# Down projections of a two-layer decoder trunk: the high weight part multiplies both halves of y in one matmul, and VectorE adds two sums

## The chip, the cores and the metric

The kernel runs on one core of one Trainium2 chip. The metric is the device time of one launch in microseconds. Three runs of the kernel before took 623.03, 623.33 and 623.62 us: the median is 623.33 us. One execution more was taken with the hardware profiler; it took 622.74 us, of which 620.9 us are the span that the profile shows.

## The reference

The program computes two decoder layers over 256 positions of width 1024, all in 32-bit floating point, and a final RMS norm. Layer 0 mixes with block-sparse attention beside gated linear attention, layer 1 with a recurrent block. Each layer ends with the same feed-forward block, which is what the change touches:

```python
def conv_ffn(x, w_up, conv_w, conv_b, w_down):
    h = causal_dwconv(x @ w_up, conv_w, conv_b)
    u, g = jnp.split(h, 2, axis=-1)
    return (u * jax.nn.gelu(g)) @ w_down

h = h + conv_ffn(rms_norm(h, ffn_norm_g[l]), ffn_w_up[l], ffn_conv_w[l], ffn_conv_b[l], ffn_w_down[l])
```

The widths are 1024 into 6144 (`w_up`), and 3072 into 1024 (`w_down`). The product with `w_down` is called the down projection here.

## The kernel before

**Layout.** Activations are kept transposed: features on the 128 partitions, the 256 positions along the free dimension. `h`, the residual stream, is 8 blocks of 128 features by 256 positions.

**Products in two halves.** TensorE is fed operands of the type fp32r. Every operand a is split in a high half, the value rounded to that type, and a low half, a minus the high half. A product a·b is taken as high·high + high·low + low·high, all summed in one PSUM region. For weights, `issue_w` (L130) loads a chunk of 128 x 1024 values (eight blocks of 128 x 128) by DMA into a tile `w`; ScalarE copies it to `wh` (L145), and VectorE subtracts into `wl` (L146). For the activations of the down projection, `Y` (L667) holds 24 blocks `y`, each with its high half [.., 0, ..] beside its low half [.., 1, ..], 256 columns each. `passes` (L152) issues three matmuls for each block: `wh` with the high half, `wh` with the low half, `wl` with the high half (L157). Each matmul instruction carries its own load of the 128 x 128 weights.

**Chunks.** 204 chunks are consumed in a fixed order. Tiles `w` have 4 buffers, so that a load waits until VectorE has made the `wl` of an earlier chunk; `wh` and `wl` have 6 buffers each, so that a split waits until TensorE has used up an earlier chunk. The first ten chunks of the recurrent block (L1_C0, NPRE) have buffers of their own and are split ahead, while the down projection of layer 0 still runs.

**The down projection** (L690 to L700) runs over m, the 8 blocks of output features. Each m takes a PSUM bank `psd` of 512 columns, uses 256 of them, and sums 3 chunks of 8 blocks into it: 72 matmuls. Then `residual` (L224) lets VectorE add the bank to block m of `h` (L225), ScalarE take squares of the block for the next norm (L183) and write the high half of the next operand `x` (L219), and VectorE the low half (L220).

**The order.** Python only gives a priority. The order on each engine is made when the kernel is built, by a scheduler that goes by a timeline of its own, and each engine runs its queue in that order: what stands behind a waiting instruction waits with it. In the recurrent block that follows layer 0, TensorE first multiplies `x` into the banks `psx` (L717).

Of the kernel before, what the change touches and what calls it, by code (L numbers as in the profile page):

```python
# [22 lines left out]
P = 128  # L23
S = 256
D = 1024
KT = 8
# [36 lines left out]
def trunk(ctx: ExitStack, tc: tile.TileContext, xT, w, wgk, wgk2, vec, cst, mskf, out):  # L63
    nc = tc.nc
# [7 lines left out]
    def bank(name, tag="g"):  # L72
        return pp.tile([P, 512], F32, tag=tag, bufs=BANKS[tag], name=name)
# [7 lines left out]
    h = big[:, 0:KT * S].rearrange("p (k t) -> p k t", k=KT)  # L81
# [4 lines left out]
    def V(name, i):  # L86
        o = VOFF[name] + i
        return vt[:, o:o + 1]
# [8 lines left out]
    def use(name):  # L97
        if tbl["name"] != name:
            ld = nc.scalar.preload_act_table_set(name)  # L99
            for o in tbl["ops"]:  # L100
                order(o, ld)
            if tbl["load"] is not None and not tbl["ops"]:
                order(tbl["load"], ld)
            tbl.update(name=name, load=ld, ops=[])

    def act(name, *args, **kw):
        use(name)
        ins = nc.scalar.activation(*args, **kw)  # L108
        order(tbl["load"], ins)
        tbl["ops"].append(ins)  # L110
        return ins

    first = []
    state = {"hooks": {}, "i": 0, "q": []}
# [10 lines left out]
    def load_w():  # L125
        while len(state["q"]) <= LOOK and state["i"] < NCH:
            state["q"].append(issue_w())
        return state["q"].pop(0)

    def issue_w():  # L130
        i = state["i"]
        state["i"] += 1
        wt = wp.tile([P, CW + 32], F32, tag="w", name=f"w{i}")[:, 0:CW]
        dma = nc.sync.dma_start(wt, w[i])
        if i == 0:
            first.append(dma)
        pre = "p" if L1_C0 <= i < L1_C0 + NPRE else ""
        nb = NPRE if pre else 6
        oh, ol = 16, 16
        wh = wp.tile([P, CW + 32], F32R, tag="wh" + pre, bufs=nb, name=f"wh{i}")[:, oh:oh + CW]  # L140
        wl = wp.tile([P, CW + 32], F32R, tag="wl" + pre, bufs=nb, name=f"wl{i}")[:, ol:ol + CW]
        nsp = 2 if i < 2 else 1
        for f in range(nsp):
            cs = slice(f * CW // nsp, (f + 1) * CW // nsp)
            hi = nc.scalar.activation(wh[:, cs], wt[:, cs], AF.Copy)  # L145
            lo = nc.vector.tensor_sub(wl[:, cs], wt[:, cs], wh[:, cs].bitcast(F32))  # L146
        for kind, o in (("h", hi), ("l", lo)):
            for before in state["hooks"].pop((kind, i), []):
                order(before, o)
        return wh, wl  # L150

    def passes(ps, ops, first=True, last=True, skip=False):  # L152
        n = len(ops)
        out = []
        for i, (ah, al, bh, bl) in enumerate(ops):
            for j, (a, b) in enumerate(((ah, bh), (ah, bl), (al, bh))):
                out.append(nc.tensor.matmul(ps, a, b, start=first and i + j == 0, stop=last and i == n - 1 and j == 2,  # L157
                                            skip_group_check=skip))
        return out

    def gemm(ps, wc, X, k0=0, first=True, last=True, nk=KT, skip=False):
        return passes(ps, [(wc[0][:, k * P:(k + 1) * P], wc[1][:, k * P:(k + 1) * P], X[:, k0 + k, 0, :], X[:, k0 + k, 1, :])
                    for k in range(nk)], first, last, skip)

    def split(hi, lo, src):
        nc.scalar.activation(hi, src, AF.Copy)
        nc.vector.tensor_sub(lo, src, hi.bitcast(F32))  # L167

    def new_x():
        return xp.tile([P, KT, 2, S], F32R, tag="x", name="x")  # L170
# [122 lines left out]
    X = new_x()  # L293
# [8 lines left out]
    with tc.tile_pool(name="l0", bufs=1) as lp, tc.tile_pool(name="l0r", bufs=4) as lr:  # L302
# [50 lines left out]
        for n, (k, i) in enumerate(seq):  # L353
            mc = 32 - 16 * i
            nc.tensor.matmul(psg[0:mc, :S], gw[:, k, 0:mc], X[:, k, i, :], start=n == 0, stop=n == 2 * KT - 1,
                             skip_group_check=True)
# [27 lines left out]
        for wdt in (64, 16, 4):  # L384
            c = cum[wdt]
# [16 lines left out]
        ps = bank("psbq")  # L402
# [18 lines left out]
        ps = bank("psbk")  # L421
# [94 lines left out]
        for nm in ("q", "k"):  # L516
            for m in range(2):
                ps = bank("psa")
# [63 lines left out]
        for pr in range(4):  # L582
            for j, ps in enumerate(scores(pr)):
                PT[2 * pr + j] = softmax(ps)
            ps = bank("pso", "t")
            for j in range(2):
                hd = 2 * pr + j
                r = slice(64 * j, 64 * j + 64)
                cs = slice(64 * hd, 64 * hd + 64)
# [11 lines left out]
        for pr in range(4):  # L601
            ps = bank("pob", "l")
            for j in range(2):
# [3 lines left out]
                cs = slice(64 * hd, 64 * hd + 64)  # L607
# [9 lines left out]
        for m in range(4):  # L617
            ps = bank("psog")
# [23 lines left out]
        X = new_x()  # L642
# [21 lines left out]
    def ffn(layer, X, norm, nextg):  # L664
        rs = norm.rstd()
        with tc.tile_pool(name=f"f{layer}", bufs=1) as yp, tc.tile_pool(name=f"f{layer}r", bufs=3) as fr:
            Y = yp.tile([P, 24, 2, S], F32R, name="y2")  # L667
            for m in range(24):
                ps = bank("psu")
                for j in range(2):  # L670
                    gemm(ps[:, j * S:(j + 1) * S], load_w(), X)
                v = fr.tile([P, 2, S], F32, tag="v", name="v")
                nc.vector.tensor_mul(v, ps.rearrange("p (j t) -> p j t", j=2), rs[:, None, :].to_broadcast([P, 2, S]))  # L673
                c = fr.tile([P, 2, S], F32, tag="c", name="c")
                for j in range(2):
                    ch = j * 24 + m
                    wv = lambda tap: V("fc_w", layer * 144 + tap * 48 + ch)
                    nc.scalar.activation(c[:, j, :], v[:, j, :], AF.Identity, bias=V("fc_b", layer * 48 + ch), scale=wv(2))  # L678
                    for d in (1, 2):
                        nc.vector.scalar_tensor_tensor(c[:, j, d:], v[:, j, 0:S - d], wv(2 - d), c[:, j, d:],  # L680
                                                       op0=ALU.mult, op1=ALU.add)
                gl = fr.tile([P, S], F32, tag="gl", name="gl")
                act(GELU, gl, c[:, 1, :], AF.Gelu_apprx_tanh)
                y = fr.tile([P, S], F32, tag="y", name="y")
                nc.vector.tensor_mul(y, c[:, 0, :], gl)
                split(Y[:, m, 0, :], Y[:, m, 1, :], y)
            use(SQRT)
            Xn = new_x() if nextg else None
            nn = Norm(last=nextg is None)
            for m in range(KT):  # L690
                ps = bank("psd")
                for c in range(3):
                    state["last"] = gemm(ps[:, :S], load_w(), Y, k0=8 * c, first=c == 0, last=c == 2)[-1]
                add = residual(ps[:, :S], m, Xn, nextg[0] if nextg else None, nextg[1] if nextg else 0, nn)
                if nextg and m == 0:
                    decay_const(add[0])
                if nextg and m == KT - 1:
                    j = loaded()
                    for kind, d, o in zip("lhl", (9, 10, 10), add):
                        ahead(kind, j + d, o)  # L700
            return Xn, nn

    X, norm = ffn(0, X, norm, ("mix_g", 1))


    rs = norm.rstd()
    with tc.tile_pool(name="l1", bufs=1) as lp, tc.tile_pool(name="l1r", bufs=3) as lr:
# [5 lines left out]
        Y = new_m("r")  # L713
# [201 lines left out]
```

## Time and profile before

| what | value |
|---|---|
| median of three runs | 623.33 us |
| profiled execution, its time | 622.74 us |
| its span | 620.9 us |
| down projection of layer 0 on TensorE | 265.7 to 330.8 us |
| recurrent block on TensorE | 330.9 to 414.2 us |
| down projection of layer 1 on TensorE | 547.3 to 612.3 us |
| matmuls `psd` in both | 1152 |

Engines are PE (TensorE's matmuls), PEld (its weight loads, which overlap the matmuls), DVE (VectorE), ACT (ScalarE), POOL and SP, whose queue issues the weight DMAs. A matmul's duration in the profile includes the time that it spends in the array; since matmuls are pipelined, the distance between two starts is what one costs. A row's bracket gives the idle time of the engine before it and what ended it.

### The profile page before, as it was taken

Reading aid. Unit: us, or ns where it says so; the run is one execution under the profiler, and the core shown is the slowest. Engines: PE = TensorE matmul, PEld = TensorE weight load, DVE = VectorE, ACT = ScalarE, POOL = GpSimd, SP = SyncE. Lnnn points to the kernel's source line nnn. Section 1 sums busy time; section 2 is a strip of 40 time slices with the busy share of each in tenths; the row PEclk is TensorE's granted clock in tenths of the full one; section 3 lists DMA queues with packets and bytes.
Section 4 is the critical chain, followed back from the end, with each engine's and each line's share of the span. In section 5 each row is a group of like instructions: output and inputs, shape, how many; then the busy total and the mean of one; then the engine's idle time right before and its main releaser. Section 6 shows DMA issues by size and latency. Waiting matters only on the chain.

```text
span 620.9 us, 13046 instructions
## 1 busy us (share of the span) xinstructions
PE 607.5 (98%) x5218; PEld 595.1 (96%) x5218; DVE 508.0 (82%) x895; ACT 416.3 (67%) x678; POOL 13.6 (2%) x42
## 2 busy tenths in 40 slices
PE   8999999999999999999998999999999999999996
PEld 5999988999999999999998999999999999999995
DVE  6699994687999999978567869797999999986541
ACT  7899575666677667675555589966767766773421
POOL 7000000000000000000000000000000000000000
PEclk9999999999999999999998999999999999999998
DMA  8662731337565555547576505467466555556501
GB/s 319 228 207 109 244 115 35 128 111 246 174 219 182 198 199 189 192 169 232 185 246 236 188 2 174 132 223 229 172 207 207 191 200 201 188 189 204 202 3 69
DMA packets 31516, 110.90 MB, mean 179 GB/s; under 512 B 3648, under 2 KB 4192, under 8 KB 31456
## 3 DMA queue, kind: packets, MB, share of 16 engines
q1 hardware_dynamic: 31168, 109.98, 51.7%
q8 instruction: 41, 0.67, 0.4%
q14 instruction: 19, 0.16, 0.1%
q10 hardware_dynamic: 288, 0.09, 0.1%
HBM read 109.01 MB, written 1.05 MB: 177 GB/s over the span
## 4 chain that ended last, share of the span: by engine, by line
PE 78%; ACT 10%; DMA 5%; DVE 4%; issue 1%; DVEq 0%; SPq 0%; ACTq 0%
PE psu L157 42%; PE psd L157 17%; DMA w<-w 4%; ACT wh L145 4%; PE psa L157 4%; PE pst L157 4%; PE psout L157 3%; ACT L99 2%; DVE wl L146 2%; PE psog L157 1%; DVE xc L724 1%; PE psbq L410 1%; PE psbk L157 1%; DMA big<-xT 1%; ACT tt L108 1%
## 5 line engine op out<-in xcount | busy, mean ns | idle before, releaser
L145 ACT ACTIVATE wh<-w 128x1024 fp32r<-128x1024 f32 (+1 forms) x206 | 214.9, 1051 | 133.6 <-PE psu L157 67.0
L146 DVE TENSOR_TENSOR wl<-w,wh 128x1024 fp32r<-128x1024 f32 (+1 forms) x206 | 248.6, 1212 | 56.1 <-ACT wh L145 53.0
L157 PE MATMUL psu<-x,wh 128*128 128x256 f32 x1536 | 263.2, 277 | 0.7 <-ACT wh L145 0.6
L157 PEld LDWEIGHTS psu<-x,wh 128*128 128x128 f32 x1536 | 231.6, 188 | 1.3 <-ACT wh L145 0.8
L157 PE MATMUL psu<-x,wl 128*128 128x256 f32 x768 | 211.8, 276 | 0.0
L157 PEld LDWEIGHTS psu<-x,wl 128*128 128x128 f32 x768 | 144.0, 188 | 0.0
L157 PE MATMUL psd<-y,wh 128*128 128x256 f32 x768 | 130.5, 276 | 0.0
L157 PEld LDWEIGHTS psd<-y,wh 128*128 128x128 f32 x768 | 115.3, 188 | 0.0
L157 PE MATMUL psd<-y,wl 128*128 128x256 f32 x384 | 105.6, 276 | 0.0
L680 DVE SCALAR_TENSOR_TENSOR c<-v,big,c 128x255 f32<-128x255 f32 (+1 forms) x192 | 84.6, 479 | 0.0
L157 PEld LDWEIGHTS psd<-y,wl 128*128 128x128 f32 x384 | 71.9, 188 | 0.0
L678 ACT ACTIVATE c<-v,big 128x256 f32<-128x256 f32 x96 | 51.6, 590 | 2.9 <-DVE v L673 2.5
L673 DVE TENSOR_TENSOR v<-psu,rs 128x512 f32<-128x512 f32 x48 | 32.5, 685 | 0.0
L183 ACT ACTIVATE sq<-big 128x256 f32<-128x256 f32 x40 | 15.5, 405 | 22.3 <-DVE big L225 21.3
L157 PE MATMUL psx<-x,wh 128*128 128x256 f32 x128 | 24.1, 290 | 2.2 <-ACT x L219 2.2
L157 PE MATMUL psout<-m,wh 128*128 128x256 f32 x128 | 23.9, 285 | 0.3 <-DVE m L167 0.3
L157 PE MATMUL pst<-wh,x 128*128 128x256 f32 x128 | 23.9, 284 | 0.0
L157 PE MATMUL psout<-r,wh 128*128 128x256 f32 x128 | 22.6, 280 | 1.1 <-ACT r L768 1.0
L157 PEld LDWEIGHTS psx<-x,wh 128*128 128x128 f32 x128 | 20.7, 199 | 2.4 <-ACT x L219 2.4
L157 PE MATMUL psa<-x,wh 128*128 128x256 f32 x128 | 23.0, 282 | 0.0
L225 DVE TENSOR_TENSOR big<-big,psd 128x256 f32<-128x256 f32 x16 | 6.7, 420 | 19.5 <-PE psd L157 19.4
L99 ACT ACT_TABLE_LOAD x17 | 21.8, 1283 | 1.0 <-PEq L905 0.7
(203 smaller groups left out, 834.4 us busy)
## 6 DMA issues: line engine op xcount, KB each, us to landing
w<-w SPq DMA_DIRECT2D x204, 512.0 KB, 3.9
big<-xT SPq DMA_DIRECT2D x4, 256.0 KB, 4.3
out<-o SPq DMA_DIRECT2D x4, 256.0 KB, 2.6
ct<-cst SPq DMA_DIRECT2D x1, 384.0 KB, 7.2
big<-vec SPq DMA_DIRECT2D x1, 224.0 KB, 7.0
mf<-mskf SPq DMA_DIRECT2D x1, 192.0 KB, 5.0
wg<-wgk ACTq DMA_DIRECT2D x1, 64.0 KB, 4.4
big<-cst SPq DMA_DIRECT2D x1, 64.0 KB, 7.0
```

What stands on the lines that cost most here:

```text
L99: ld = nc.scalar.preload_act_table_set(name)
L108: ins = nc.scalar.activation(*args, **kw)
L145: hi = nc.scalar.activation(wh[:, cs], wt[:, cs], AF.Copy)
L146: lo = nc.vector.tensor_sub(wl[:, cs], wt[:, cs], wh[:, cs].bitcast(F32))
L157: out.append(nc.tensor.matmul(ps, a, b, start=first and i + j == 0, stop=last and i == n - 1 and j == 2, skip_group_check=skip))
L183: ins = nc.scalar.activation(sq, t, AF.Square)
L225: add = nc.vector.tensor_add(h[:, m, :], h[:, m, :], ps)
L410: seq = [nc.tensor.matmul(ps[:, hf * S:(hf + 1) * S], a, b, start=n == 0, stop=n == 23) for n, (a, b) in enumerate(mms)]
L673: nc.vector.tensor_mul(v, ps.rearrange("p (j t) -> p j t", j=2), rs[:, None, :].to_broadcast([P, 2, S]))
L678: nc.scalar.activation(c[:, j, :], v[:, j, :], AF.Identity, bias=V("fc_b", layer * 48 + ch), scale=wv(2))
L680: nc.vector.scalar_tensor_tensor(c[:, j, d:], v[:, j, 0:S - d], wv(2 - d), c[:, j, d:], op0=ALU.mult, op1=ALU.add)
L724: nc.vector.scalar_tensor_tensor(xc[n][:, j, d:], v[:, j, 0:S - d], V("rc_w", (3 - d) * 8 + m), xc[n][:, j, d:], op0=ALU.mult, op1=ALU.add)
```

## The change

A new helper `wide` replaces `gemm` in the down projections alone. For each block it issues one matmul of `wh` with 512 columns, the high and the low half of `y` as one operand, into the whole bank, and one matmul of `wl` with the high half into columns 256 to 511. So the first half of the bank ends as high·high, the second as high·low + low·high. VectorE adds the second half to `h` in an instruction of its own (L705 of the changed kernel), ahead of the one in `residual` that adds the first half. Nothing else of the program's text differs.

```diff
+    def wide(ps, wc, X, k0=0, first=True, last=True):
+
+        out = []
+        for k in range(KT):
+            cs = slice(k * P, (k + 1) * P)
+            out.append(nc.tensor.matmul(ps, wc[0][:, cs], X[:, k0 + k].rearrange("p h t -> p (h t)"),
+                                        start=first and k == 0, stop=False, skip_group_check=True))
+            out.append(nc.tensor.matmul(ps[:, S:], wc[1][:, cs], X[:, k0 + k, 0, :], start=False,
+                                        stop=last and k == KT - 1, skip_group_check=True))
+        return out
...
-                    state["last"] = gemm(ps[:, :S], load_w(), Y, k0=8 * c, first=c == 0, last=c == 2)[-1]
+                    state["last"] = wide(ps, load_w(), Y, k0=8 * c, first=c == 0, last=c == 2)[-1]
+                nc.vector.tensor_add(h[:, m, :], h[:, m, :], ps[:, S:])
                 add = residual(ps[:, :S], m, Xn, nextg[0] if nextg else None, nextg[1] if nextg else 0, nn)
```

On TensorE the last blocks of a down projection read as follows before (`x2` means two such instructions in a row).

```order
L157 MATMUL psd<-y_1842,wh_4410 128x256 x2
L157 MATMUL psd<-y_1842,wl_4411 128x256
L157 MATMUL psd<-y_1842,wh_4410 128x256 x2
L157 MATMUL psd<-y_1842,wl_4411 128x256
L157 MATMUL psd<-y_1842,wh_4410 128x256 x2
L157 MATMUL psd<-y_1842,wl_4411 128x256
```

And on TensorE at the same place now.

```order
L170 MATMUL psd<-y_1842,wh_4241 128x512
L172 MATMUL psd<-y_1842,wl_4242 128x256
L170 MATMUL psd<-y_1842,wh_4241 128x512
L172 MATMUL psd<-y_1842,wl_4242 128x256
L170 MATMUL psd<-y_1842,wh_4241 128x512
L172 MATMUL psd<-y_1842,wl_4242 128x256
```

Three instructions have become two, 384 times over both layers: 1152 matmuls become 768, and the columns streamed stay 768 for each block.

On VectorE, at the end of the down projection of layer 0, before: the row L225 is the add of the last block, m = 7; the `wl` rows are splits of weight chunks of the recurrent block. `wl_4880` is the chunk that was loaded as number 114 (counted from 0), `wl_4923` number 115, `wl_4790` number 112.

```order
L146 TENSOR_TENSOR wl_4752<-w_4749,wh_4751 128x1024
L146 TENSOR_TENSOR wl_4880<-w_4877,wh_4879 128x1024
L225 TENSOR_TENSOR big<-big,psd 128x256
L146 TENSOR_TENSOR wl_4790<-w_4787,wh_4789 128x1024
L146 TENSOR_TENSOR wl_4923<-w_4920,wh_4922 128x1024
L190 TENSOR_TENSOR ssq<-ssq,sq 128x256
```

On VectorE at the same place now: L705 is the new add, L236 the old one; `wl_4696` is number 114, `wl_4739` number 115, `wl_4606` number 112.

```order
L146 TENSOR_TENSOR wl_4696<-w_4693,wh_4695 128x1024
L705 TENSOR_TENSOR big<-big,psd 128x256
L146 TENSOR_TENSOR wl_4739<-w_4736,wh_4738 128x1024
L236 TENSOR_TENSOR big<-big,psd 128x256
L146 TENSOR_TENSOR wl_4606<-w_4603,wh_4605 128x1024
L201 TENSOR_TENSOR ssq<-ssq,sq 128x256
```

The old add of block 7 stood behind the split of chunk 114; now it stands behind the new add and the split of chunk 115 as well. For blocks 5 and 6 a split stands between the two adds too; for blocks 3 and 4 they stand side by side.

On TensorE, the first matmuls `psx` of the recurrent block, before: the first row is two matmuls of the second chunk. `wh_4440` in the second row is the first matmul that reads block 7 of `x`; 35 matmuls `psx` stand ahead of it.

```order
L157 MATMUL psx<-x,wh_4563 128x256 x2
L157 MATMUL psx<-x,wh_4440 128x256
L157 MATMUL psx<-x,wl_4564 128x256
L157 MATMUL psx<-x,wh_4563 128x256 x2
L157 MATMUL psx<-x,wl_4564 128x256
```

On TensorE at the same place now: `wh_4263` in the fourth row is the first matmul that reads block 7.

```order
L157 MATMUL psx<-x,wh_4452 128x256 x2
L157 MATMUL psx<-x,wl_4453 128x256
L157 MATMUL psx<-x,wh_4452 128x256
L157 MATMUL psx<-x,wh_4263 128x256
L157 MATMUL psx<-x,wh_4379 128x256
```

49 matmuls `psx` now stand ahead of the first that reads block 7: 21 of one chunk, 21 of a second and 7 of a third.

## Rows read from the trace of the kernel before

**Rows 1.** The page: busy us (share of the span) and instructions of each engine.
```profile
PE 607.5 (98%) x5218; PEld 595.1 (96%) x5218; DVE 508.0 (82%) x895; ACT 416.3 (67%) x678; POOL 13.6 (2%) x42
```

**Rows 2.** Windows: us, busy us of PE, PEld, DVE, ACT, POOL, PEclk, DMA share, GB/s.
```profile
265.70:331.00 65.30, 65.30 (x579) 65.30 (x578) 47.90 (x83) 38.12 (x49) 0.00 (x0) 1.00 0.64 210
337.00:340.40 3.40, 3.16 (x15) 3.17 (x16) 3.40 (x5) 2.07 (x3) 0.00 (x0) 0.50 0.81 265
345.00:390.00 45.00, 45.00 (x399) 45.00 (x398) 39.27 (x66) 35.88 (x58) 0.20 (x2) 1.00 0.34 112
375.00:405.00 30.00, 28.91 (x252) 28.51 (x252) 25.76 (x35) 29.25 (x41) 0.20 (x2) 1.00 0.46 155
```

**Rows 3.** The chain that ended last: start us, us, engine, tile, line, count.
```profile
57.67 0.43 PE pa L478 x2
58.57 0.86 PE pss L555 x8
...
416.28 10.65 PE psu L157 x89
...
547.30 65.28 PE psd L157 x576
612.58 0.87 PE pot L800 x8
```

**Rows 4.** Timeline of layer 0's down projection: start us, us, engine, line, out<-in, count.
```profile
302.19 0.30 PEld L157 LDWEIGHTS psd<-y,wh 128*128 128x128 f32 x2
302.30 0.39 PE L157 MATMUL psd<-y,wh 128*128 128x256 f32 x2
302.42 0.19 PEld L157 LDWEIGHTS psd<-y,wl 128*128 128x128 f32 x1
302.53 0.28 PE L157 MATMUL psd<-y,wl 128*128 128x256 f32 x1
```

**Rows 5.** Timeline of the program's end.
```profile
612.62 0.42 DVE L225 TENSOR_TENSOR big<-big,psd 128x256 f32<-128x256 f32 x1 [6.57 <-PE psd L157]
613.07 0.42 ACT L183 ACTIVATE sq<-big 128x256 f32<-128x256 f32 x1 [7.75 <-DVE big L225]
613.18 0.30 PEld L199 LDWEIGHTS nps<-big,ssq 128*128 128x128 f32 x2
613.54 0.38 PE L199 MATMUL nps<-big,sq 128*128 128x1 f32 x2
```

**Rows 6.** Timeline of ACT and DVE as layer 0 passes into the recurrent block.
```profile
309.19 1.06 ACT L145 ACTIVATE wh<-w 128x1024 fp32r<-128x1024 f32 x1 [0.95 <-PE psd L157]
313.09 2.01 ACT L145 ACTIVATE wh<-w 128x1024 fp32r<-128x1024 f32 x2 [2.85 <-DMA w<-w]
...
333.62 1.06 ACT L145 ACTIVATE wh<-w 128x1024 fp32r<-128x1024 f32 x1 [2.73 <-DMA w<-w]
334.72 1.23 DVE L146 TENSOR_TENSOR wl<-w,wh 128x1024 fp32r<-128x1024 f32 x1 [4.34 <-ACT wh L145]
335.20 1.06 ACT L145 ACTIVATE wh<-w 128x1024 fp32r<-128x1024 f32 x1 [0.52 <-DMA w<-w]
335.86 0.41 DVE L225 TENSOR_TENSOR big<-big,psd 128x256 f32<-128x256 f32 x1
336.69 0.49 ACT L219 ACTIVATE x<-big 128x256 fp32r<-128x256 f32 x1
```

**Rows 7.** Timeline of PE at the same place.
```profile
330.86 0.39 PE L157 MATMUL psx<-x,wh 128*128 128x256 f32 x2
...
334.60 0.39 PE L157 MATMUL psx<-x,wh 128*128 128x256 f32 x2
337.24 0.58 PE L157 MATMUL psx<-x,wh 128*128 128x256 f32 x1 [2.25 <-ACT x L219]
```

**Rows 8.** Waits over the whole run: engine, line, for whom; us in total, times, longest.
```profile
ACT wh L145 <- DMA w<-w: 24.0, 19, 4.5
```

**Rows 9.** The page's groups: line, engine, tiles, count | busy us, mean ns.
```profile
L225 DVE TENSOR_TENSOR big<-big,psd 128x256 f32<-128x256 f32 x16 | 6.7, 420 | 19.5 <-PE psd L157 19.4
```

## The prediction

> **What bounds the kernel now.** I read the page first: TensorE is busy for 98% of the span and its weight loads for 96%, ScalarE and VectorE for 67% and 82% [rows 1]. So a change in what TensorE issues counts, unless another engine ends the stage. The windows then say where that holds. In the down projection of layer 0 and from 345 to 390 us TensorE has no gap at all, and the clock is granted in full, 2.4 GHz; from 375 to 405 us it idles 1.1 us while ScalarE works 29.25 of 30 us [rows 2]. The chain confirms it for the down projection of layer 1: 576 matmuls in one unbroken piece of 65.28 us [rows 3], 113.3 ns each. For layer 0 the windows count the same length, but the chain there turns from TensorE to weight DMAs near 309 us, and the timeline shows why: at 309.19 a split on ScalarE still waits for TensorE to free a buffer, at 313.09 and 333.62 splits wait for a DMA [rows 6]. The split of the waiting chunk holds VectorE for 4.34 us, and the add of block 7 stands behind it [rows 6]. TensorE runs 35 matmuls of the recurrent block (330.86 to 334.7, every 0.113 us) and then idles 2.25 us for block 7 of x [rows 7]; it goes on at half clock, 0.50 or 1.2 GHz, until about 340.4 [rows 2].
>
> **What a block of the down projection costs, before and now.** Before, one block is three matmuls: its two wh matmuls start at 302.30, its wl one at 302.53, and 65.28 / 576 x 3 makes 340 ns a block [rows 3, 4]. Two weight loads in a row last 0.30 us together where one lasts 0.19, so they follow each other every 0.11 us [rows 4]. At the program's end two loads ahead of matmuls of a single column also take 0.30 us [rows 5]. A matmul of one column thus paces no faster than one of 256, and I conclude that it is the load of 128 x 128 weights, about 111 to 113 ns, that sets the pace. Now a block is one matmul of 512 columns and one of 256. No fp32r matmul of 512 columns is in the trace. The nearest row is a plain f32 matmul of 256 columns, which goes through the array as two instructions of double length: 0.43 us for two, 215 ns each, with a load for each [rows 3]. That is 512 columns' worth of array time with its load hidden. The other matmul still has to wait for the next wh load behind it: 113 ns. So 215 + 113 = 328 ns, 12 ns less than 340.
>
> Bounds: if a 512-column matmul costs two of 256 (226.6 ns), the block stays at 340 and nothing is gained. If the short matmul goes at the 109 ns of the closing transposes (0.87 us for eight) [rows 3], the block takes 324 and the gain is 16 ns. Should the wide operand read worse than two separate ones, there would be a loss; I know no row for that and give it half the gain's size, 6 ns, as an estimate. I take 12, the value of the row with the same array time.
>
> Each layer has 192 blocks: 192 x 12 = 2.3 us per layer, with bounds +1.2 (loss) and -3.1.
>
> A rule that speaks against so much: the Trainium skill ("TensorE: Matmul & The Clock Gate", Back-to-back issue gap) gives an isolated warm matmul N / 2.4 + 2.5 ns. By it a block would go from 3 x 109.2 = 327.5 to 215.8 + 109.2 = 325 ns, a gain of 2.5 ns, or 1 us in both layers. The trace agrees for the long one, 215, and not for the short, 113 where the rule has 109; so I let the row decide.
>
> **Layer 1, the program's end.** Nothing but TensorE is late there, so the whole 2.3 us arrive. But the last bank needs two adds, in order, on the same block of h. The add after the last matmul runs from 612.62 for 0.42 us, the squares follow at 613.07, and the matmul on them at 613.54, with TensorE waiting [rows 5]. The second add puts 0.42 us on this path [rows 9]. Its bounds are 0.3 and 0.5 us. The other seven adds are hidden: VectorE idled 6.57 us before the last one [rows 5]. Layer 1: -2.3 + 0.4 = -1.9 us.
>
> **Layer 0, the passage into the recurrent block.** TensorE gets through its 192 blocks 2.3 us earlier, so at 328.5 instead of 330.8. It then has 49 matmuls instead of 35 that don't need block 7: 14 x 0.113 = 1.6 us more. It comes to the wait at 328.5 + 49 x 0.113 = 334.1, where before it came at 334.8.
>
> When does block 7 come? Up to the split at 309.19 the chunks go at TensorE's pace: 16 of the 24 chunks are through, so everything behind is earlier by 16/24 of 2.3, 1.5 us. From then on DMA, split and subtraction follow each other at the same pace as before. Against that, the old add now stands behind one more add (0.42) and one more subtraction (1.23) [rows 6, 9]: 1.65 us later. That subtraction, of chunk 115, needs a split that before ran from 335.20 after a DMA wait of 0.52 us [rows 6]; 1.5 us earlier it ends at 334.8, just as the one of chunk 114 is done, so it adds no wait of its own. Sum: +0.2 us. Block 7 lets TensorE go at about 337.4, after an idle time of some 3.3 us instead of 2.25, but with 14 matmuls more behind it. TensorE is then 1.6 - 0.2 = 1.4 us ahead of before. The half clock after the wait is taken as long as before (3.4 us of the window with 0.50 [rows 2]); it could be gone 1.5 us earlier or later, at half the speed worth about 0.8 us.
>
> From there to 390 us TensorE has no gap [rows 2], and ScalarE and VectorE, whose splits are also about 1.4 us earlier, feed on its banks. ScalarE has no slack from 375 to 405 us [rows 2], and the end of the recurrent block waits for it. The scheduler has put nine matmuls more of the projections ahead of the first gates (about 1 us in one place), with one of ScalarE's splits taken out of a later place. I take 1.0 us of the 1.4 as arriving. Bounds: -2.3, all that TensorE gained, and +1.0, where the adds' 1.65 us count in full and the DMAs are no earlier, of which the 14 matmuls take back part.
>
> The sum against the profiled execution, 622.74 us: -2.3 + 0.4 - 1.0 = -2.9, so 619.9 us. The median of the runs is 0.59 us above that execution, so I forecast 620.5 us for it.
>
> **Rivals.**
>
> *Swallowed in layer 0.* What TensorE wins there is a longer wait for block 7, since DMA and VectorE set its time. For it: TensorE already waits there, and the wait grows in my own sum. Against: the DMAs up to 309 us hang on TensorE's pace. The shift is 0 to +0.8 instead of -1.0; the time is 623.33 - 1.9 + 0.4 = 621.8, between 621.4 and 622.2.
>
> *A fixed cost for each instruction.* Loads don't pace the matmuls; each instruction has its columns' time and a small extra. Then 384 instructions fewer are all that is won. The gap from 113.3 to the 107.5 of eight short f32 matmuls (0.86 us for eight) [rows 3] is 5.8 ns: 1.1 us per layer. The shift in layer 0 falls to about -0.3. Time: 623.33 - 1.1 + 0.4 - 0.3 = 622.3. For it: 113 and 109 lie close. Against: the one-column matmuls. The issue-gap rule of the Trainium skill (TensorE: Matmul & The Clock Gate) is of this kind with 2.5 ns an instruction, and by it the time would be 623.33 - 1.0 + 0.4 - 0.2 = 622.5.
>
> *Time goes by columns.* 768 columns before and after, 340 ns before and after. The tail's 0.4 stays, the passage is about +0.1, since 14 matmuls cover 1.6 of the adds' 1.65. Time 623.8, no change. For it: the columns are the same. Against: 215 ns for the long f32 instruction, less than 2 x 113.
>
> *A late DMA between the two adds: slower.* The last add of layer 0 now stands behind the split of chunk 115, which waits for its DMA. ScalarE's longest wait for a weight DMA is 4.5 us, and 19 such waits make 24.0 us [rows 8]. If one of that size falls on chunk 115, TensorE idles 4.5 us more, and the half clock lasts longer, 0.8 us. Time: 620.5 + 5.3 = 625.8. It decides from the point where block 7 comes more than 4 us later than in my sum. Against: the DMA of chunk 115 was 0.52 us late before [rows 6], and the chunk loads come from the same queue in the same order.
>
> **How the numbers follow.** Two kernels can be told apart here from about 0.2%, 1.25 us, so faster means below 622.1 and slower above 624.6. Forecast: 0.53, of which 0.51 faster. Swallowed: 0.17, of which 0.11 faster. Fixed cost: 0.13, of which 0.04 faster. Columns: 0.09, same. Late DMA or a wide matmul that loses: 0.08, slower. Together faster 0.66, same 0.26, slower 0.08. The forecast's own range is 618.5 (16 ns a block and a shift of -2.1 in layer 0) to 621.6. For 8 in 10 I go from 618.5 up to 623.2: this takes in swallowed and fixed cost, and leaves out columns and the slower case.
>
> **What the profile will show.** Right if the 512-column matmuls of layer 1 stand with 384 instructions in about 63.0 us instead of 65.28, and the starts in a block lie 0.215 and 0.113 us apart; if VectorE has two adds of 0.42 us in a row at the end, with the squares 0.4 us further from the last matmul; and if TensorE waits for block 7 at about 334, for some 3.3 us, with layer 1's first psu matmuls about 1.0 us ahead of 416.3 [rows 3]. The columns rival is shown by 0.226 us for a long matmul, the fixed cost by 0.220 with 0.108, the swallowed gain by layer 1's first psu matmul at or after 416.3. A wait of 7 us or more before block 7 would be the slower case. The forecast is wrong if the piece of layer 1 stays above 64.5 us, or if the time gained there is found missing elsewhere.

## The result: slower, and where the time went

The changed kernel took 627.26 us, median of six runs (625.59 to 627.9), beside 623.18 us for the kernel before on the same chip. The ratio is 1.0062, with a 95% interval of 1.0046 to 1.0078: 2.9 to 4.9 us slower, outside the range that was forecast and on the other side of zero. The profiled execution took 627.9 us, with a span of 626.1 us; it is the slowest of the six.

A span can be cut at four places that every kernel here has in common: the first matmul `psd` of each layer, the first `psx` behind layer 0's down projection, and the first `pot` behind layer 1's. The pieces are differences of those starts in the trace, in us, one profiled execution for each kernel. The names of the lower rows are those of the experiments below.

| kernel | before layer 0's psd | psd, layer 0 | between | psd, layer 1 | tail | span |
|---|---|---|---|---|---|---|
| before | 265.58 | 65.28 | 216.27 | 65.29 | 8.53 | 620.9 |
| after | 265.46 | 66.79 | 217.90 | 66.99 | 8.93 | 626.1 |
| e1_two_sums | 264.90 | 65.28 | 218.34 | 65.28 | 8.99 | 622.8 |
| e2_layer1_only | 265.54 | 65.28 | 216.44 | 67.19 | 8.94 | 623.4 |
| e3_grouped | 264.98 | 66.26 | 216.52 | 66.30 | 8.93 | 623.0 |
| e4_root_first | 266.83 | 66.79 | 214.72 | 67.00 | 8.91 | 624.2 |
| e6_add_first | 264.95 | 65.28 | 213.51 | 65.28 | 8.52 | 617.5 |
| e7_wide_add_first | 265.73 | 66.79 | 212.95 | 67.00 | 8.92 | 621.4 |

So the loss of 5.1 us between the two profiled executions is +1.5 and +1.7 in the down projections, +0.4 in the tail and +1.6 between the layers. The piece between the layers holds all of the recurrent block and the up projection of layer 1, and is the one that varies most. The first column lies ahead of everything that was changed and still goes from 264.90 to 266.83, so a difference of less than 2 us outside the down projections says little when it comes from one execution.

### The profile page after: what moved, and what is told of

Same layout as the page of the kernel before. It is cut to its first block, busy times and chain, and to the rows that moved or that the text cites. A ratio compares the mean times of both kernels' runs of the same rounds, so it can differ in the third digit from the quotient of the medians.

```text
span 626.1 us, 12305 instructions
## 1 busy us (share of the span) xinstructions
PE 610.1 (97%) x4834; PEld 581.7 (93%) x4834; DVE 513.3 (82%) x911; ACT 416.6 (67%) x678; POOL 12.8 (2%) x42
## 4 chain that ended last, share of the span: by engine, by line
PE 79%; ACT 9%; DVE 5%; DMA 4%; issue 2%; DVEq 0%; ACTq 0%; SPq 0%
PE psu L157 42%; PE psd L170 12%; PE psd L172 6%; DMA w<-w 4%; PE psa L157 4%; PE pst L157 4%; ACT wh L145 4%; PE psout L157 3%; PE psog L157 2%; DVE xc L736 2%; ACT L99 2%; DVE wl L146 2%; PE psbk L157 1%; PE psbq L421 1%; PE pl L509 1%
## 5 line engine op out<-in xcount | busy, mean ns | idle before, releaser
L170 PE MATMUL psd<-y,wh 128*128 128x512 f32 x384 | 133.7, 393 | 0.0
L172 PE MATMUL psd<-y,wl 128*128 128x256 f32 x384 | 107.1, 280 | 0.0
L170 PEld LDWEIGHTS psd<-y,wh 128*128 128x128 f32 x384 | 72.1, 188 | 16.1
L705 DVE TENSOR_TENSOR big<-big,psd 128x256 f32<-128x256 f32 x16 | 6.7, 419 | 22.7 <-PE psd L172 22.7
L157 PE MATMUL psx<-x,wh 128*128 128x256 f32 x128 | 22.8, 279 | 1.2 <-ACT x L230 1.2
L157 PEld LDWEIGHTS psout<-r,wh 128*128 128x128 f32 x128 | 20.4, 200 | 2.3 <-ACT r L780 2.3
```

Of the source, the lines that this page charges most:

```text
L170: out.append(nc.tensor.matmul(ps, wc[0][:, cs], X[:, k0 + k].rearrange("p h t -> p (h t)"), start=first and k == 0, stop=False, skip_group ...
L172: out.append(nc.tensor.matmul(ps[:, S:], wc[1][:, cs], X[:, k0 + k, 0, :], start=False, stop=last and k == KT - 1, skip_group_check=True))
L705: nc.vector.tensor_add(h[:, m, :], h[:, m, :], ps[:, S:])
```

## The profile after

The page of the changed kernel has 384 matmuls fewer than [rows 1], yet TensorE is busy for 2.6 us more:

```profile
PE 610.1 (97%) x4834; PEld 581.7 (93%) x4834; DVE 513.3 (82%) x911; ACT 416.6 (67%) x678; POOL 12.8 (2%) x42
```

The windows of the two down projections (columns as in [rows 2]) show that this is no idle time: TensorE is busy from end to end, at the full clock, and its weight loads are busy for 8 us less than the matmuls. Before, both were busy throughout [rows 2]. The loads have slack now, and the matmuls still take longer:

```profile
265.46:332.25 66.79, 66.79 (x386) 58.67 (x385) 50.09 (x91) 38.43 (x49) 0.00 (x0) 1.00 0.64 210
550.15:617.14 66.99, 66.99 (x386) 58.75 (x385) 37.61 (x60) 25.58 (x33) 0.00 (x0) 1.00 0.37 126
```

66.99 us over 192 blocks are 349 ns a block, where 340 were spent before [rows 3] and 328 were forecast. The timeline of layer 1 (start us, us) shows the parts, as [rows 4] did before. A long matmul is followed by the short one 0.23 us later, and that by the next long one after 0.12 us. Over all 384 blocks the distances between starts are 230.5 and 117.9 ns on average: 348.4 together.

```profile
591.02 0.39 PE L170 MATMUL psd<-y,wh 128*128 128x512 f32 x1
591.25 0.28 PE L172 MATMUL psd<-y,wl 128*128 128x256 f32 x1
591.37 0.39 PE L170 MATMUL psd<-y,wh 128*128 128x512 f32 x1
591.60 0.28 PE L172 MATMUL psd<-y,wl 128*128 128x256 f32 x1
```

The end of the program, beside [rows 5]: two adds of 0.42 us stand in a row, and the squares start 0.91 us behind the start of the first add. Before they started 0.45 us behind the only one, so this path is 0.46 us longer.

```profile
617.02 0.28 PE L172 MATMUL psd<-y,wl 128*128 128x256 f32 x1
...
617.34 0.42 DVE L705 TENSOR_TENSOR big<-big,psd 128x256 f32<-128x256 f32 x1 [6.33 <-PE psd L172]
617.80 0.42 DVE L236 TENSOR_TENSOR big<-big,psd 128x256 f32<-128x256 f32 x1
618.25 0.42 ACT L194 ACTIVATE sq<-big 128x256 f32<-128x256 f32 x1 [7.96 <-DVE big L236]
```

The page's group of the new adds, beside [rows 9], has the same duration:

```profile
L705 DVE TENSOR_TENSOR big<-big,psd 128x256 f32<-128x256 f32 x16 | 6.7, 419 | 22.7 <-PE psd L172 22.7
```

The passage into the recurrent block, beside [rows 6, 7], first on TensorE. The wait for block 7 of `x` has shrunk from 2.25 to 1.21 us. A second wait is new: 2.41 us for `rtk`, the norm's factors for the recurrent block. A third, at 404.75 for ScalarE, is longer than before.

```profile
339.22 0.62 PE L157 MATMUL psx<-x,wh 128*128 128x256 f32 x3 [1.21 <-ACT x L230]
...
347.98 0.43 PE L217 MATMUL nps<-big,rtk 128*128 128x128 f32 x2 [2.41 <-DVE rtk L216]
...
404.75 1.01 PE L157 MATMUL psout<-r,wh 128*128 128x256 f32 x3 [2.11 <-ACT r L780]
```

In the kernel before, that third wait took 1.0 us (waits: us in total, times, longest):

```profile
PE psout L157 <- ACT r L768: 1.0, 1, 1.0
```

Block 7 comes late by two steps. On VectorE the new add runs at 336.38, 0.5 us later than the only add did before (335.86) [rows 6], and the old one 1.47 us behind it, with the split of chunk 115 between them:

```profile
336.38 0.41 DVE L705 TENSOR_TENSOR big<-big,psd 128x256 f32<-128x256 f32 x1
...
337.85 0.41 DVE L236 TENSOR_TENSOR big<-big,psd 128x256 f32<-128x256 f32 x1
```

On ScalarE the square root behind `rtk` (L108) stands behind a split that waits 2.33 us for its DMA:

```profile
345.53 1.06 ACT L145 ACTIVATE wh<-w 128x1024 fp32r<-128x1024 f32 x1 [2.33 <-DMA w<-w]
346.49 0.24 ACT L108 ACTIVATE rtk<-nps,big 128x2 f32<-128x2 f32 x1
```

In the kernel before, the same square root ran at 342.87, and only the splits behind it came later:

```profile
342.87 0.24 ACT L108 ACTIVATE rtk<-nps,big 128x2 f32<-128x2 f32 x1
343.13 1.28 ACT L99 ACT_TABLE_LOAD   x1
344.42 2.01 ACT L145 ACTIVATE wh<-w 128x1024 fp32r<-128x1024 f32 x2
```

The windows add the clock. It stays full after the wait for block 7, where the kernel before ran at 0.50, which is 1.2 GHz [rows 2]. Instead it falls to 0.50 behind the wait at 404.75:

```profile
337.00:340.40 3.40, 2.19 (x19) 2.00 (x19) 3.38 (x6) 2.05 (x4) 0.00 (x0) 1.00 0.73 241
404.70:408.10 3.40, 3.35 (x15) 3.34 (x16) 2.60 (x4) 2.41 (x3) 0.00 (x0) 0.50 0.00 0
```

The waits of splits for weight DMAs did not grow over the whole run, beside [rows 8]; one of them only stands at a worse place.

```profile
ACT wh L145 <- DMA w<-w: 21.2, 15, 4.3
```

## The experiments

Three questions: is it the wide operand or the second sum that costs; what does a matmul of so many columns cost by itself; and what does the order in the passage cost. Ratios are to the kernel before, run on the same chip.

**The wide operand alone.** e1_two_sums keeps the two sums and both adds, but issues the 512 columns as two matmuls of 256:

```diff
-            out.append(nc.tensor.matmul(ps, wc[0][:, cs], X[:, k0 + k].rearrange("p h t -> p (h t)"), ...
+            out.append(nc.tensor.matmul(ps[:, :S], wc[0][:, cs], X[:, k0 + k, 0, :], ...
+            out.append(nc.tensor.matmul(ps[:, S:], wc[0][:, cs], X[:, k0 + k, 1, :], ...
...
```

> Three matmuls of 256 columns for each block as before, but the two low products are summed in the second half of the bank and VectorE adds that half in an instruction of its own, as in the changed kernel. If the operand of 512 columns is what slows a block (347 ns after, 340 before), a block is back at 340 ns, layer 1's down projection at 65.3 us instead of 67.0, and of the 3.9 us lost only the tail's 0.4 to 0.5 us and what the new order in the passage costs stay: 623.5 to 624.5 us. If the second sum (its half of the bank, its adds) is what slows TensorE, the block stays near 347 ns and the time near 627.

625.11 us against 622.96, ratio 1.0033 [1.0019, 1.0047]. The windows of its two down projections:

```profile
264.90:330.18 65.28, 65.28 (x578) 65.28 (x577) 49.79 (x91) 38.11 (x49) 0.00 (x0) 1.00 0.66 211
548.52:613.80 65.28, 65.28 (x578) 65.28 (x577) 37.79 (x60) 25.71 (x33) 0.00 (x0) 1.00 0.40 130
```

65.28 us again, to the hundredth. So the wide operand is what makes a block longer, and not the second sum. The tail keeps its extra 0.46 us, which is the second add. The time is higher than these two would make it, and than the 623.5 to 624.5 us expected. The table says where: 2.1 us more between the layers. The wait for block 7 is not longer than before, 2.30 beside 2.25 us [rows 7]. Of the 2.1 us, 1.1 lie in the later wait for ScalarE, which took 1.0 before; the rest is not taken apart here:

```profile
338.09 0.72 PE L157 MATMUL psx<-x,wh 128*128 128x256 f32 x4 [2.30 <-ACT x L234]
```

```profile
PE psout L157 <- ACT r L784: 2.1, 1, 2.1
```

**Layer 1 alone.** e2_layer1_only takes `wide` and the extra add in layer 1 and `gemm` in layer 0. The program's text for layer 0 and for the passage is then that of the kernel before.

```diff
-                    state["last"] = wide(ps, load_w(), Y, k0=8 * c, first=c == 0, last=c == 2)[-1]
-                nc.vector.tensor_add(h[:, m, :], h[:, m, :], ps[:, S:])
+                    if layer:
+                        state["last"] = wide(ps, load_w(), Y, k0=8 * c, first=c == 0, last=c == 2)[-1]
+                    else:
+                        state["last"] = gemm(ps[:, :S], load_w(), Y, k0=8 * c, first=c == 0, last=c == 2)[-1]
+                if layer:
+                    nc.vector.tensor_add(h[:, m, :], h[:, m, :], ps[:, S:])
```

> The change in layer 1 alone; layer 0 and the passage into the recurrent block are as before. If each down projection loses 1.5 to 1.7 us by itself, the time is that of before + 1.7 + 0.4 = 625.3 us, and TensorE waits for block 7 of x for 2.25 us as before. If most of the loss came from the passage, it is within 0.8 us of before: 623.2 to 624.

625.05 us against 622.96, ratio 1.0032 [1.0015, 1.0049]: +2.1 us. In one execution it has both costs of a block side by side, 65.28 us in layer 0 and 67.19 in layer 1:

```profile
265.54:330.82 65.28, 65.28 (x578) 65.28 (x577) 48.10 (x84) 38.18 (x49) 0.00 (x0) 1.00 0.68 215
547.26:614.45 67.19, 67.19 (x387) 58.88 (x385) 37.60 (x60) 25.59 (x33) 0.00 (x0) 1.00 0.40 126
```

+1.9 for the blocks and +0.4 for the tail make 2.3; the runs have 2.1. The layer where nothing but TensorE was late was to bring 1.9 us, and costs 2.1. The wait for block 7 was expected at 2.25 us and is 1.82; another 1.25 us go to `rtk`, the clock stays full, and the piece between the layers is 216.44 us, as before.

**The order in the passage.** e4_root_first is the changed kernel with the norm's square root asked to stand ahead of the split of chunk 118. The same argument puts the reciprocal behind the root ahead of that chunk's `wl`, and the copy of the factors ahead of the split of chunk 119:

```diff
-    rs = norm.rstd()
+    rs = norm.rstd(hook=118)
```

> The changed kernel, but ScalarE's square root for the norm is ordered ahead of the split of weight chunk 118, as it stands in the kernel before. If the wait of 2.4 us that TensorE has near 345.5 us is due to that root standing behind a split that waits for a DMA, the wait falls below 0.5 us and the time by 1.5 to 2.4 us, to 625 to 626 us. If the weights are late anyway and ScalarE bounds the recurrent block, the wait moves to a later place and the time stays at 627.

626.03 us against 622.96, ratio 1.0047 [1.003, 1.0064]: at the upper edge of what was expected. TensorE's wait for `rtk` falls from 2.41 to 0.66 us, where less than 0.5 was expected:

```profile
345.60 0.43 PE L217 MATMUL nps<-big,rtk 128*128 128x128 f32 x2 [0.66 <-DVE rtk L216]
```

The piece between the layers falls by 3.2 us in the profiled execution, and the median, set against its own kernel before, by 1.0 (from +4.1 to +3.1 us). So the trace shows that the root's place makes most of that wait. What it is worth in time the runs do not settle: the intervals of the two losses, 2.9 to 4.9 and 1.9 to 4.0 us, overlap. The down projections stay at 66.79 and 67.00 us.

**The pace of a matmul by itself.** e5_paces is the kernel before with series of 24 matmuls each behind its last down projection, on the same `y` and `wh`:

```diff
...
+                series = [[256] * 24, [512] * 24, [512, 256] * 12, [384] * 24, [0] * 24, [-256] * 24]
...
```

(0 and −256 stand for 512 and 256 columns of bf16 operands; their weights and columns come from one tile of zeros, each matmul with its own load.)

> The kernel before, with six series of 24 matmuls each after the last down projection, into banks that nothing reads, each with its own weight load: fp32r of 256 columns, of 512, of 512 and 256 in turn, of 384, then bf16 of 512 and of 256. If the load of the weights sets 113 ns (my prediction), 512 columns take 215, 384 take 162 and the pair 328. If fp32r columns are streamed at 113/256 = 0.44 ns each, 512 take 226, 384 take 170 and the pair 340, while bf16 columns, half as wide, go at 215 for 512. If changing between long and short matmuls costs by itself, only the series in turn shows more than the sum of its parts: 347 instead of 340.

The windows of the first three series, the matmuls of the series alone (us, then busy us of PE and PEld, the clock, DMA; a count can include the neighbour at an edge):

```profile
611.22:613.93 2.71, 2.71 (x24) 2.71 (x25) 1.00 0.00 0
613.93:619.53 5.60, 5.60 (x26) 4.52 (x25) 1.00 0.00 0
619.53:623.77 4.24, 4.24 (x26) 3.68 (x24) 1.00 0.00 0
```

2.71 us for 24 of 256 columns are 113 ns each, as in the kernel. 5.60 us for 24 of 512 are 233 ns each, not 215. 4.24 us for twelve pairs are 353 ns a pair, worse than 233 + 113. Matmuls of 384 columns start 171 to 178 ns apart. With bf16 operands the distances are 215.8 ns for 512 columns and 109.2 for 256: here two short ones cost 2.6 ns more than a long one, and in fp32r 7 ns less. The weight loads, 4.52 of 5.60 us busy, are not what the long matmul waits for.

**Long ones and short ones apart.** e3_grouped issues in each chunk the eight long matmuls first, then the eight short ones, chained in this order:

```diff
+        for k in range(KT):
+            cs = slice(k * P, (k + 1) * P)
             out.append(nc.tensor.matmul(ps[:, S:], wc[1][:, cs], X[:, k0 + k, 0, :], ...
+        for a_, b_ in zip(out, out[1:]):
+            order(a_, b_)
```

> The changed kernel with the matmuls of a chunk in another order: eight of 512 columns, then eight of 256. If changing between long and short costs (118 ns for a short one behind a long one, 113 among its own), the short ones fall to 113 ns and a chunk from 2.78 us to at most 2.77 us, with the long ones at 233 ns as in the series; if the long ones are slow by themselves, as that series says, nothing is gained: 2.77 to 2.81 us a chunk, a down projection of 66.5 to 67.4 us, the time 626.5 to 628.

625.19 us against 623.23, ratio 1.0033 [1.0016, 1.0049]: below the 626.5 to 628 us expected, which counted 233 ns for a long matmul. Its chain of waits in layer 1 shows the groups:

```profile
594.94 1.83 PE psd L170 x8
596.77 0.94 PE psd L174 x8
```

Here eight long ones take 1.83 us, 229 ns each, and over all groups eight short ones 0.91 to 0.94 us, 114 to 118 ns each. A down projection takes 66.3 us: 0.5 to 0.7 us less than in the changed kernel, 1.0 more than before. So grouping takes back 0.5 to 0.7 of the 1.5 to 1.7 us. Taking turns is part of the loss, and a long fp32r matmul among its like still costs more than two short ones.

**Which part of a matmul sets its pace.** Two more kernels, e8_paces2 and e9_paces3, have series like those of e5_paces. Each entry is columns, weight columns, and a third number (in e8, 0 keeps one block of `y` for the whole series; in e9, 1 writes to two banks in turn and 2 keeps one weight tile):

```diff
...
+                series = [(256, 128, 1), (256, 32, 1), (512, 32, 1), (512, 128, 0), (224, 128, 1), (288, 128, 1)]
...
+                series = [(224, 32, 0), (128, 128, 0), (128, 32, 0), (448, 128, 0), (512, 128, 1), (512, 128, 2)]
...
```

> The kernel before with six other series of 24 fp32r matmuls after the last down projection: 256 columns with 128 x 128 weights, 256 columns with 128 x 32 weights, 512 columns with 128 x 32 weights, 512 columns with 128 x 128 weights and the same moving operand each time, then 224 and 288 columns with 128 x 128 weights. If the load of the weights paces 256 columns, 32 weight columns let them go at 107 to 109 ns, and 224 columns stay at 111 to 113. If the columns pace them, 32 weight columns leave 113, 224 take 99 to 111, 288 take 127 to 133. If it is the weight load beside it that slows the long operand (231 to 236 ns where 2 x 113 is 226), the narrow weights bring 512 columns to 226 or less; if it is the reading of the operand itself, it stays at 231 to 236.

> The kernel before with six series of 24 fp32r matmuls behind its last down projection: 224 columns with 128x32 weights; 128 columns with 128x128 weights; 128 columns with 128x32 weights; 448 columns; 512 columns written in turn to two banks; 512 columns with one and the same weight tile each time. Theory A, columns at about 0.44 ns with a floor from the weight load: 128 columns with 128x128 weights still go every 110 to 112 ns, as the 224 columns did (111.6), and with 32 columns of weights the floor falls, so that 224 go at 99 to 102 ns and 128 at 57 to 80. Theory B, no floor from the load: 224 columns cost 111.6 whatever the weights, 128 columns a good deal less than 111 with either. For 448 columns 198 to 205 ns by both (0.443 to 0.457 ns a column). For the long ones: if what makes 512 columns cost 229 to 236 instead of 226.6 is that matmuls in a row write the same bank, two banks in turn bring 226 to 227; if it is the change of weights, one tile brings it; else both stay at 229 to 236.

The windows of e8's six series:

```profile
614.31:617.03 2.72, 2.72 (x24) 2.72 (x25) 1.00 0.00 0
617.03:619.75 2.72, 2.72 (x26) 2.59 (x24) 1.00 0.00 0
619.75:625.30 5.55, 5.55 (x27) 2.67 (x25) 1.00 0.00 0
625.30:630.80 5.50, 5.50 (x26) 4.51 (x24) 1.00 0.00 0
630.80:633.47 2.67, 2.67 (x26) 2.67 (x24) 1.00 0.00 0
633.47:636.64 3.17, 3.17 (x26) 3.10 (x24) 1.00 0.03 5
```

And of e9's six:

```profile
612.84:615.34 2.50, 2.50 (x24) 2.49 (x24) 1.00 0.00 0
615.34:617.98 2.64, 2.64 (x26) 2.64 (x25) 1.00 0.00 0
617.98:619.42 1.44, 1.44 (x27) 1.44 (x26) 1.00 0.00 0
619.42:624.28 4.86, 4.86 (x28) 4.56 (x26) 1.00 0.00 0
624.28:629.77 5.49, 5.49 (x26) 4.51 (x24) 1.00 0.01 3
629.77:635.26 5.49, 5.49 (x25) 4.32 (x23) 1.00 0.00 0
```

Each length divided by 24 is nearly the cost of one matmul. The first distance of a series still depends on its neighbour (71 ns between the first two of 128 columns with wide weights), so the table has the mean of the others:

| columns | weights 128 x 128 | weights 128 x 32 |
|---|---|---|
| 128 | 112 ns | 60 ns |
| 224 | 112 ns | 104 ns |
| 256 | 113 ns | 113 ns |
| 288 | 132 ns | |
| 448 | 200 ns | |
| 512 | 229 ns | 231 ns |

Read down the middle column: 128 and 224 columns cost the same, 111.7 and 111.8 ns, so something else than columns sets the pace there, and it is gone when the weights are narrower. There is a floor that goes with the width of the weights, as a floor from their load would. (Narrow weights also write 32 rows of the bank instead of 128; no run separates the two.) But 256 columns cost 113.3 ns with wide and with narrow weights: they lie just above the floor, and there the columns set the pace. The two limits are less than 2 ns apart at 256 columns, and at 256 and 512 narrower weights gain nothing. The floor is one of fp32r: in e5 bf16 matmuls of 256 columns, with weights of 128 columns, go at 109 ns. The Trainium skill ("TensorE: Matmul & The Clock Gate", LDWEIGHTS) gives a load a time that grows with its weight columns alone, by its formula an estimate of 106.7 ns for 128 columns. The floor that these series show is 5 ns higher.

The other widths put the question of the long matmul in another light. A column costs 0.466 ns at 224 (narrow weights), 0.457 at 288, 0.447 at 448 and at 512, and 0.443 at 256. So 512 columns are not out of line with their neighbours; it is 256 among their like that are the cheapest of all fp32r widths measured.

For the few ns that the long ones lose beyond 226.6, two banks in turn and one and the same weight tile leave 229, as one block of `y` leaves 229 to 230. None of the three is the cause. The series of e5, in which block and weights changed and the bank did not, had 233; whether the 4 ns come from there or from another chip is not shown.

**The order alone.** What the trace of the kernel before shows of the passage could be mended there without the change. e6_add_first is the kernel before, with two more orders: the high half of `x` of block 7 ahead of the split of chunk 114, its low half ahead of that chunk's `wl`. The add, which both of them read, moves ahead with them.

```diff
-                    for kind, d, o in zip("lhl", (9, 10, 10), add):
+                    for kind, d, o in zip("lhlhl", (9, 10, 10, 11, 11), [add[0], add[1], add[2], add[1], add[2]]):
```

> The kernel before, with the last block's add, its high half and low half of x ordered ahead of the splits of chunks 112 to 114 in the passage. If the 2.25 us of idle time and the half clock that follows come from the add standing behind a split that waits for a DMA, TensorE's wait falls below 0.5 us, the clock stays full and up to 3 us are gained: 620 to 622. If ScalarE's chain of splits and activations sets the end of the recurrent block whatever TensorE does, the time stays at 623.

619.58 us against 623.23, ratio 0.9956 [0.9942, 0.997]: faster by 3.65 us, the best kernel here, and a little below the 620 to 622 us expected. The add of block 7 now waits for TensorE alone and runs at 330.43, where it ran at 335.86 before [rows 6]; `x` follows at 331.27. A window over the first 67 us of the recurrent block has the clock in full and TensorE idle for 1.4 us in all.

```profile
330.43 0.42 DVE L225 TENSOR_TENSOR big<-big,psd 128x256 f32<-128x256 f32 x1 [0.59 <-PE psd L157]
...
331.27 0.49 ACT L219 ACTIVATE x<-big 128x256 fp32r<-128x256 f32 x1
```

```profile
330.50:398.00 67.50, 66.07 (x583) 65.87 (x582) 56.38 (x88) 56.33 (x83) 0.41 (x4) 1.00 0.45 147
```

e7_wide_add_first puts the same two orders and those of e4_root_first into the changed kernel.

> The changed kernel with both its waits of the passage taken away: the adds of block 7 ordered ahead of the splits of chunks 112 to 114, the square root ahead of the split of chunk 118. If the change costs 1.5 to 1.7 us in each down projection and 0.45 us at the end whatever the passage does, it stays 3.5 to 4 us behind the run of the kernel before with the same order: 624 to 625.5. If my prediction's sum failed mainly by the passage, it comes to 622 or less.

623.31 us against 623.23, ratio 1.0005 [0.9992, 1.0019]: no difference to the kernel before. This is less than the 624 to 625.5 us expected, since e6 gained more than expected; the distance to e6 is the expected one. Its passage has no wait either; the window of 334.0 to 348.2 us has TensorE busy throughout, where the changed kernel had waited twice:

```profile
334.00:348.20 14.20, 14.20 (x127) 14.20 (x127) 11.55 (x15) 11.29 (x16) 0.00 (x0) 1.00 0.80 264
```

Between e6 and e7 only the change differs, and the passage is clean in both: 3.73 us by the medians. The table's pieces give 1.5 + 1.7 + 0.4 = 3.6. This is what the change costs by itself, and of the changed kernel's 4.1 us it leaves 0.3 to 0.5 for the passage, which is within the noise. The parts do not simply add up: e1, whose blocks cost what they did before, loses 2.15 us by its median, of which 0.46 are the tail, so some 1.7 lie between the layers. Layer 0's late blocks and its late passage overlap: together they cost 2.0 us, the changed kernel's 4.1 less e2's 2.1.

## Why the prediction was wrong, step by step

**The step that failed: that the load of 128 x 128 weights sets the pace, so that a block takes 215 + 113 = 328 ns.** It rested on [rows 3 to 5], and they were read for more than they show. The one-column matmuls [rows 5] show a floor of the load, 0.11 us; e8 and e9 show such a floor, 112 ns. That it binds at 256 columns too was a conclusion from two numbers lying close, 111 and 113. The two limits happen to cross there, and the columns are the upper one (e8: 113 ns with 32 weight columns). The 215 ns of the plain f32 matmul [rows 3] were taken for 512 columns' worth of array time. It reads 256 columns of the operand and passes twice; it says nothing of reading 512 fp32r columns, which take 229 to 233. And the 113 ns for the short one became 118, since it now stands behind a long one. The kernel before had a row that speaks against the step: the gates' matmuls (timeline of TensorE; eight with 32 weight columns and eight with 16, 256 columns each) start (2.03 - 0.28) / 15 = 0.117 us apart, no faster than with 128 weight columns.

```profile
7.12 2.03 PE L355 MATMUL psg<-x,gw 128*32 128x256 f32 x16 [0.77 <-DVE gw L279]
```

Sum: 230.5 + 117.9 in place of 215 + 113: +8.4 ns a block against 340, where -12 was forecast. Over 192 blocks this is +1.6 us per layer (measured +1.5 and +1.7) instead of -2.3.

**The bounds.** A loss of 6 ns was kept as the lower bound, an estimate without a row; the loss was 8.4. The sentence said that a wide operand might read worse than two, and gave it part of 0.08. It is what happened.

**The rule weighed against it.** The issue gap of the Trainium skill ("TensorE: Matmul & The Clock Gate", Back-to-back issue gap), N / 2.4 + 2.5 ns, makes 325 ns a block, an estimate by its figures. In e5 it holds to the nanosecond for bf16, 215.8 and 109.2, and not for fp32r, 233 and 113. The agreement of the 215 ns with it was taken as support in the prediction; but that was not a row of an fp32r matmul. The rival's 622.5 us by that rule counts both layers' 1.0 us and then layer 0 once more in the shift; with layer 1's 0.5 the sum would be 623.0.

**Layer 1 and the tail.** That all of a block's time arrives there was right; it arrived with the other sign. The second add on the path, +0.4, was right: +0.40 in the piece, 0.46 to the squares. The hidden adds were hidden.

**The passage, -1.0 forecast.** TensorE came to the wait for block 7 at 338.0 instead of 334.1, since its 192 blocks were done 1.4 us later than before and not 2.3 earlier. The 49 matmuls ahead of the wait did their work: the wait was 1.21 us, shorter than before, and the clock stayed full. Block 7 came at 339.2, 2 us later than before, where +0.2 was forecast. The two adds with a split between them cost 1.5 us, close to the 1.65 of the sum; but the split ahead of them came 0.5 us later, where the sum had it 1.5 earlier by TensorE's gain. What was missed is the next step: on ScalarE the square root of the norm moved behind the split of chunk 118, and so behind its DMA. The prediction followed the queues up to the splits that carry block 7 and stopped there. TensorE's wait for the root was 2.41 us in this execution; e4's medians put it at 1.0 us, not clear of the noise. The passage as a whole made +1.6 us in this execution, 0.3 to 0.5 by the medians of e6 and e7.

**The rivals.** *Time goes by columns* (623.8) was the nearest in mechanism: columns do set the pace at 256, with block 340, tail 0.4, passage about 0. It was too kind by 8.4 ns a block, 3.2 us. *A late DMA between the two adds* (625.8) has the nearest time and is not what happened: no wait of that size stood before block 7. Its kind of event, an engine's needed instruction queued behind a split that waits for a DMA, occurred one step later, on ScalarE. That its figure lies so near is luck. *Swallowed in layer 0* and *A fixed cost for each instruction* both needed a gain on TensorE, and there was none.

**What stays open.** Why long fp32r matmuls cost 229 to 233 ns instead of 226.6, and why a short one beside a long one costs 118. The runs exclude the weight load, a change of the block of `y`, of the bank and of the weight tile. They do not exclude the place of an operand in memory, and one reading speaks for it. In the changed kernel 36 of the 48 chunks take 346 to 349 ns a block and 12 take 351 to 355, and they are the same 12 in e4 and e7, whose times differ. In layer 0 they are every sixth chunk, and `wh` and `wl` have six buffers. Four slow chunks in layer 0 and eight in layer 1 are also why the two down projections lose 1.5 and 1.7 us. No run moved a buffer. Open, too, is the size of the passage's part in the changed kernel.

## What to carry to other kernels

Before merging matmuls, ask of the trace which limit the short one is at, with an operation that takes only one of them away: the same columns with narrower weights. Here the trace of before held such an operation, the gates' matmuls. Two durations that lie close don't show one cause. And when a change puts another instruction into an in-order queue, follow the queue to the next thing that TensorE needs, and to the one behind it: 3.65 us lay in the place of one add and the two halves of `x` behind it, more than the whole change was to bring.

## What the runs showed of the hardware

An fp32r matmul costs 0.443 ns a column at 256 columns and 0.447 to 0.456 at 512 (113.3, 228.9 and 233.4 ns), where bf16 costs 0.421 at 512 (215.8). In fp32r one instruction of 512 columns is thus dearer than two of 256, weight loads included; in bf16 it is not. In a stream of 256 columns alone the distance is 113; where lengths take turns, the short one costs 118. In these fp32r series a matmul with 128 weight columns cost no less than 112 ns on average, however few its columns; with 32 it went down to 60.
